# A hybrid decoder trunk on one core: two sets of rotation tables, later reads of table accumulators, and three smaller reorderings

## The chip, the cores and the metric

The kernel runs on one core of a Trainium2 chip. The metric is the device time of one execution in microseconds (us). The median of three runs is 2419.24 us (2417.57 to 2420.35).

## What is computed

Two streams of tokens go through two layers that share one set of weights: a prompt (16 meta tokens and 1024 tokens) and a sample (8 sequences of 8 tokens, which bring caches). Layer 0 mixes with a diagonal complex scan (S5) beside sliding-window attention, layer 1 with a convolution module; each layer ends in a gated feed-forward block.

```python
def s5_mixer(u, h0_re, h0_im, lam_re, lam_im, log_step, b_re, b_im, c_re, c_im, d_skip, w_glu, b_glu):
    ...
    decay = jnp.exp(lr * dt)
    a_re = decay * jnp.cos(li * dt)
    a_im = decay * jnp.sin(li * dt)
    ...
    _, _, hr, hi = lax.associative_scan(_complex_affine_combine, (a_full_re, a_full_im, bu_re, bu_im), axis=1)
    y = (jnp.einsum('ntgp,gcp->ntgc', hr, c_re.astype(f32))
         - jnp.einsum('ntgp,gcp->ntgc', hi, c_im.astype(f32)))
    y = y.reshape(n, t, D_SSM) + d_skip.astype(f32) * uf
    g = jax.nn.gelu(y)
    out = g * jax.nn.sigmoid(g @ w_glu.astype(f32) + b_glu.astype(f32))
    return out.astype(u.dtype), hr[:, -1], hi[:, -1]

def trunk(x, ssm_re, ssm_im, swa_k, swa_v, conv_st, ffn_st, p):
    for layer in range(DEPTH):
        h = rmsnorm(x, p['g_mix'][layer])
        if layer % 2 == 0:
            z = h @ p['w_in_mix'][idx]
            ...  # u, q, k, v = parts of z; ya = s5_mixer(u), yb = sliding-window attention(q, k, v)
            x = x + jnp.concatenate([ya, yb.astype(ya.dtype)], axis=-1) @ p['w_out_mix'][idx]
        else:
            yc, nc = conformer_conv(h, past, ...)
            x = x + yc
        h = rmsnorm(x, p['g_ffn'][layer])
        yf, nf = conv_ffn(h, past, ...)
        x = x + yf
    return rmsnorm(x, p['g_final']), states
```

All matrices are 32-bit. The S5 part has 32 groups of 16 channels with 64 complex states each; D_MODEL is 1024.

## The kernel before

**Tiling.** The tokens stand along the free axis, 512 in stream A and 592 (528 of prompt, 64 of sample) in stream B. A projection is a row of units: one block of weight columns times one stream, summed in the accumulator `pu` (TensorE, L329). To keep 32-bit accuracy each operand is cut into a high and a low half, and each step of a unit takes three products (high by high, low by high, high by low). A weight block is loaded by SyncE into one of four `raw` buffers, its high half `whi` is made by ScalarE (L224) and its low half `wlo` by VectorE (L230), in five slots that come free as TensorE finishes with them. Units of A (inputs `a0h`, `a0l`, ...) and of B (`y0h`, ...) alternate over the same weights.

**What sets the order.** There is no scheduler: each engine does its instructions in the order in which the program was written, and waits at the head of its queue. `run` goes through the units, and after each step of a unit calls `pump`, which advances deferred stages by one tick (`chain`, `tick`) and lets background generators go some steps further, each at a rate of its own. The generators that matter here run beside the first projection (the one that makes u, q, k, v) and behind it:

- `s5_rot` makes four groups (j = 0 to 3) of rotation tables, cosine and sine of an angle. For each: GpSimd adds the angles into `tz` (L755), ScalarE takes their absolute value and two sines (L759 to L761), VectorE multiplies (L763), ScalarE squares and scales (L765, L766), and SyncE stores the two tables `tj` to the memory buffer `tD` (L768). There is one set of `tz` halves and of `tj` tables for all four groups.
- `s5_prep` makes the other tables, again for j = 0 to 3: `ee` (L834 to L839) and `ff` (L854 to L859) on VectorE, a product into the accumulator `psk` (L876) that ScalarE copies to `kz` (L880), with a diagonal that VectorE adds (L882) and a store to `mD`, and two transposes into `psf` (L890) that ScalarE copies to `xf` (L893) and SyncE stores to `xfD`.
- attention, block by block: queries come back through memory (`xB<-qD`), scores `sps` (L1246), scaled by VectorE into `xA` (L1250), maximum `mx` and `nm` (L1190, L1192), exponentials on ScalarE (L1197).
- `s5_main`, behind them: loads of `u`, `xf`, the tables `T`, `m`, `e`; `stage1` (products and a rotation), `stage2` (two scans with the decay rows `dk`, rotation back into `H`, then end states `hf` and initial states copied by ScalarE, L973 and L975), `stage3` (products into `yps`). The output goes to memory and is read back as `yrd` for the gate.

`qst` (L553) and `us` (L1425) are VectorE's reads of finished accumulators `pu`: queries and S5 channels. A third unit can start in an accumulator only when the first has been read, since there are two.

Two more places: the sample's attention multiplies by its values in two groups of four sequences (L1410 with 128 cached rows, L1411 with 8 new rows, alternating), and `start_norm` lets a background generator make the norm of a stream: after `wait` steps it forms the sums of squares (`psum_s`, L381), the reciprocal roots (L366 to L373), and spreads them (`psum_r`, L402).

Of the kernel before, what the change touches and what calls it, by code (L numbers as in the profile page):

```python
# [19 lines left out]
P = 128  # L20
# [107 lines left out]
class Trunk:  # L128
    def __init__(self, ctx, tc, a, o):
# [7 lines left out]
        self.now = self.nt = 0  # L137
# [52 lines left out]
    def bank(self, name="bk"):  # L190
        return self.psb.tile([P, 512], F32, tag="b", name=name)

# [526 lines left out]
    def s5_rot(self):  # L719
# [31 lines left out]
        y = tz[:, 0:576].rearrange("p (g q b) -> p g q b", g=4, q=9)  # L751
        c = tz[:, 576:1152].rearrange("p (g q b) -> p g q b", g=4, q=9)
        for j in range(4):
            g4 = slice(4 * j, 4 * j + 4)
            G.tensor_tensor(y, ta[:, g4, :].unsqueeze(2).to_broadcast([P, 4, 9, 16]),  # L755
                            tb[:, g4, :].unsqueeze(3).to_broadcast([P, 4, 9, 16]), op=OP.add)
            yield
            tcos, tsin = (pp.tile([P, 4, 9, 16], F32, name="tj", tag=f"tj{ri}") for ri in range(2))
            nc.scalar.activation(c, y, AF.Abs)  # L759
            nc.scalar.activation(c, c, AF.Sin, bias=hpi, scale=-1.0)  # L760
            nc.scalar.activation(tcos, y, AF.Sin)  # L761
            yield
            nc.vector.scalar_tensor_tensor(tsin, tcos, 2.0, c, op0=OP.mult, op1=OP.mult)  # L763
# [3 lines left out]
            for ri, tt in ((1, tsin), (0, tcos)):  # L767
                nc.sync.dma_start(self.dq(self.tD, ri, j, 132), tt.rearrange("p g q b -> p g (q b)")[:, :, 0:132])  # L768
# [5 lines left out]
    def s5_prep(self):  # L774
# [86 lines left out]

        nxt = table_e(0)
        yield
        for j in range(4):
# [9 lines left out]
            for gi in range(4):  # L874
                for ri in range(2):
                    nc.tensor.matmul(ps[gi * 32:(gi + 1) * 32, 0:P], bd[:, ri, gi, :],  # L876
                                     ee[:, ri, gi, 0:8, :], start=(ri == 0), stop=(ri == 1))
            z = self.t_tile(240, "kz")
            V.memset(z[:, 0:112], 0.0)
            nc.scalar.copy(z[:, 112:240], ps[:, 0:P])  # L880
            dcol = self.pc["ssm_d"] + j
            V.scalar_tensor_tensor(z[:, 112:128], mask16, self.pt[:, dcol:dcol + 1], z[:, 112:128],  # L882
                                   op0=OP.mult, op1=OP.add)
            nc.sync.dma_start(dap(self.mD, 8 * j * 16 * 8 * P, [[8 * P, P], [P, 8], [1, P]]),
                              dap(z, 0, [z.ap[0], [16, 8], [1, P]]))
            yield
            for ri in range(2):
# [5 lines left out]
                nc.scalar.copy(xf, ps)  # L893
                nc.sync.dma_start(dap(self.xfD, ri * 16 * P + 4 * j * P, [[32 * P, P], [1, 512]]), xf)
                yield


    def s5_main(self, gA):
# [15 lines left out]
        for i in range(2):  # L914
            nc.gpsimd.memset(d_(i)[:, :, 0:1], 0.0)
# [95 lines left out]
        for i in range(10):  # L1011
# [15 lines left out]
            if i >= 2:  # L1027
                load_m(i)
                load(i, e_, self.eD, P)
# [1060 lines left out]
```

## Time and profile before

| | before |
|---|---|
| median of three runs | 2419.24 us |
| profiled execution | 2420.04 us |
| its span | 2418.3 us |
| TensorE (PE) busy | 2319.7 us, 96% |
| VectorE (DVE) busy | 1662.1 us, 69% |
| ScalarE (ACT) busy | 995.0 us, 41% |
| GpSimd (POOL) busy | 136.9 us, 6% |
| the chain that ended last | PE 79%, DVE 10%, ACT 5%, DMA 4% |

A share of busy time is an average over the span: TensorE's is between 0.6 and 0.9 in the first eighth of it, and 0.9 or more behind. What matters is in which stretch an engine stood still, and what ended that. The mean granted TensorE clock of the whole execution is 0.977 of full speed.

### The profile page before, as it was taken

The numbers are of one execution on the slowest core, as the hardware profiler recorded it, in microseconds if no ns is written. First come the engines' busy times: TensorE is split into PE (matmuls) and PEld (weight loads), VectorE is DVE, ScalarE is ACT, GpSimd is POOL, SyncE is SP. The second block draws the span as 40 slices with busy tenths as digits, with TensorE's granted clock in tenths as the row PEclk, the third lists the DMA queues.
The fourth block names the chain that finished last, engine by engine and source line by source line (L and its number), as shares of the span: only waits on it lengthen the run. The fifth ranks groups of instructions, "written<-read, shape, count | busy, mean of one in ns | idle before, by whom it ended". The sixth has DMA issues, their size and how long they took to land.

```text
span 2418.3 us, 37176 instructions
## 1 busy us (share of the span) xinstructions
PE 2319.7 (96%) x13896; PEld 2084.7 (86%) x13896; DVE 1662.1 (69%) x3049; ACT 995.0 (41%) x1903; POOL 136.9 (6%) x380
## 2 busy tenths in 40 slices
PE   7688899999999999999999999999999999999998
PEld 5567778677887878999999999888887989999998
DVE  7768565554678688888887478898988564344443
ACT  6433444654434343423336333443335444233333
POOL 4001300000000001000000000000000000000000
PEclk8899999999999999999999999999999999999999
DMA  7777734224333423222222432333332423222222
GB/s 217 194 138 194 208 121 154 74 75 126 89 97 106 138 83 92 82 81 82 77 79 83 140 106 79 98 95 103 94 99 77 133 86 96 80 79 79 83 80 70
DMA packets 455354, 257.82 MB, mean 107 GB/s; under 512 B 57323, under 2 KB 446599, under 8 KB 453222
## 3 DMA queue, kind: packets, MB, share of 16 engines
q1 hardware_dynamic: 451990, 251.55, 36.1%
q0 software_dynamic: 2496, 2.68, 0.4%
q8 instruction: 110, 1.80, 0.3%
q10 hardware_dynamic: 688, 1.21, 0.1%
q14 instruction: 70, 0.57, 0.1%
HBM read 223.05 MB, written 35.59 MB: 107 GB/s over the span
## 4 chain that ended last, share of the span: by engine, by line
PE 79%; DVE 10%; ACT 5%; DMA 4%; issue 2%; SPq 0%; ACTq 0%; POOL 0%; DVEq 0%
PE pu L329 75%; DVE wlo L230 2%; DMA yrd<-yD 1%; ACT whi L224 1%; PE tps L1233 1%; DVE xB L1686 1%; DMA raw<-in_w_in_mix 1%; ACT P L1197 1%; DVE mx L1190 1%; PE sps L1246 0%; DVE hf L417 0%; DMA xbD<-xB 0%; PE psum_s L381 0%; PE ops L1260 0%; DVE cv L1517 0%
## 5 line engine op out<-in xcount | busy, mean ns | idle before, releaser
L230 DVE TENSOR_TENSOR wlo<-raw,whi 128x512 fp32r<-128x512 f32 x712 | 481.2, 679 | 498.6 <-ACT whi L224 486.1
L224 ACT CAST whi<-raw 128x512 fp32r<-128x512 f32 x712 | 428.4, 607 | 682.9 <-PE pu L329 630.9
L1686 DVE SCALAR_TENSOR_TENSOR xB<-gl,pt,xB 128x528 f32<-128x528 f32 x240 | 183.1, 763 | 4.3 <-ACT xB L1680 2.9
L1686 DVE SCALAR_TENSOR_TENSOR xA<-gl,pt,xA 128x512 f32<-128x512 f32 x240 | 179.0, 747 | 3.7 <-ACT xA L1680 1.5
L1506 ACT ACTIVATE cv<-cv 128x608 f32<-128x608 f32 (+2 forms) x88 | 58.9, 670 | 162.4 <-DVE cv L1505 162.4
L329 PE MATMUL pu<-a0h,whi 128*128 128x296 f32 (+3 forms) x318 | 92.4, 343 | 14.1 <-ACT G L1486 4.9
L1504 DVE SCALAR_TENSOR_TENSOR cv<-G,pt,cv 128x608 f32<-128x608 f32 (+2 forms) x88 | 70.1, 796 | 45.9 <-ACT cv L1503 45.8
L329 PE MATMUL pu<-a4h,whi 128*128 128x296 f32 (+3 forms) x306 | 88.8, 341 | 12.2 <-DVE xA L460 9.6
L329 PE MATMUL pu<-a2h,whi 128*128 128x296 f32 (+3 forms) x318 | 90.9, 339 | 0.0
L329 PE MATMUL pu<-a1h,whi 128*128 128x296 f32 (+3 forms) x318 | 90.5, 338 | 0.0
L329 PE MATMUL pu<-a3h,whi 128*128 128x296 f32 (+3 forms) x318 | 90.1, 337 | 0.0
L329 PE MATMUL pu<-a0l,whi 128*128 128x296 f32 (+3 forms) x318 | 90.1, 337 | 0.0
L329 PE MATMUL pu<-a1l,whi 128*128 128x296 f32 (+3 forms) x318 | 89.9, 336 | 0.0
L329 PE MATMUL pu<-a1h,wlo 128*128 128x296 f32 (+3 forms) x318 | 89.8, 335 | 0.0
L329 PE MATMUL pu<-a0h,wlo 128*128 128x296 f32 (+3 forms) x318 | 89.6, 335 | 0.0
L329 PE MATMUL pu<-a2h,wlo 128*128 128x296 f32 (+3 forms) x318 | 89.6, 334 | 0.0
L329 PE MATMUL pu<-a2l,whi 128*128 128x296 f32 (+3 forms) x318 | 89.5, 335 | 0.0
L329 PE MATMUL pu<-a3l,whi 128*128 128x296 f32 (+3 forms) x318 | 89.0, 333 | 0.0
L329 PE MATMUL pu<-a3h,wlo 128*128 128x296 f32 (+3 forms) x318 | 88.7, 332 | 0.0
L329 PE MATMUL pu<-a6h,whi 128*128 128x296 f32 (+3 forms) x306 | 88.2, 339 | 0.0
L329 PE MATMUL pu<-a6l,whi 128*128 128x296 f32 (+3 forms) x306 | 87.1, 336 | 0.9 <-DVE a6l L230 0.9
L329 PE MATMUL pu<-y0h,whi 128*128 128x296 f32 (+2 forms) x236 | 67.5, 342 | 21.2 <-DVE kz L882 17.2
(650 smaller groups left out, 6238.8 us busy)
## 6 DMA issues: line engine op xcount, KB each, us to landing
raw<-in_ffn_w_up SPq DMA_DIRECT2D x352, 256.0 KB, 2.9
raw<-in_ffn_w_down SPq DMA_DIRECT2D x128, 256.0 KB, 2.8
raw<-in_conv_w_pw SPq DMA_DIRECT2D x96, 256.0 KB, 2.8
raw<-in_ffn_w_down SPq DMA_DIRECT2D x64, 192.0 KB, 2.5
xbD<-xB SPq DMA_DIRECT2D x3, 2368.0 KB, 9.8
xB<-xbD SPq DMA_DIRECT2D x6, 1184.0 KB
raw<-in_w_in_mix SPq DMA_DIRECT2D x16, 256.0 KB, 5.8
raw<-in_w_in_mix SPq DMA_DIRECT2D x32, 128.0 KB, 3.5
```

The costliest lines, as they stand in the source:

```text
L224: nc.scalar.copy(hi, src)
L230: nc.vector.tensor_tensor(lo, src, hi.bitcast(F32), op=OP.subtract)
L329: nc.tensor.matmul(ps[:, ch, :c], wt, xt[:, off + ch * c:off + (ch + 1) * c], start=(k == 0 and pi == 0), stop=(k == nk - 1 and pi == 2))
L1190: V.tensor_reduce(mx, pt, axis=AX.X, op=OP.max)
L1197: nc.scalar.activation(pt[:, h, :], pt[:, h, :], AF.Exp, bias=nm[:, h:h + 1], accum_out=sm[:, h:h + 1])
L1233: nc.tensor.transpose(v[:, h, :], pt[:, 4 * kv + h, ko:ko + m], self.ident[:nq, :nq])
L1504: nc.vector.scalar_tensor_tensor(c, G[:, 1:1 + n], wc(1), c, op0=OP.mult, op1=OP.add)
L1506: self.chain(lambda: None, lambda: None, lambda: nc.scalar.activation(c, c, AF.Gelu_apprx_tanh))
L1686: V.scalar_tensor_tensor(acc, gl[:, i:i + npp], w(i), acc, op0=OP.mult, op1=OP.add)
```

## The change

Five edits.

1. `s5_rot` uses two sets of tables in turn. The sum of the angles goes into one half of `tz`, which is also where the second sine and the product end up; the cosine table is `tj0` or `tj1`, by j. ScalarE takes the first sine ahead of the absolute value. Two more steps of the generator stand in each j, so that every part of a later table comes later in the program.
2. `kz` and `xf` are copied out of their accumulators one tick later (`later_read`), and the diagonal of `kz` with its store three ticks after that. The `kz` buffers are two fixed ones, whose zeros are written once by GpSimd. `bank` lets ticks pass if a deferred read still holds an accumulator that comes round.
3. In `s5_main` the first column of `H` is zeroed once by GpSimd, the decay rows `dk` of an iteration are copied at its end, and the end states of an iteration are copied in the next one, behind `stage1`.
4. The sample's value products take the four of 128 rows first, and then the four of 8 rows.
5. The norm of B ahead of layer 0's feed-forward block waits 16 steps and not 7. It lies beside the first projection of A's convolution.

```diff
@@ bank, later_read
+        while self.held and self.nb - min(self.held) >= 4:
+            self.tick()
+        self.nb += 1
         return self.psb.tile([P, 512], F32, tag="b", name=name)
+
+    def later_read(self, lag, read, *more):
+
+        n = self.nb - 1
+        self.held.append(n)
+
+        def f():
+            read()
+            self.held.remove(n)
+        self.chain(*[lambda: None] * lag, f, *more)
@@ s5_rot
-        y = tz[:, 0:576].rearrange("p (g q b) -> p g q b", g=4, q=9)
-        c = tz[:, 576:1152].rearrange("p (g q b) -> p g q b", g=4, q=9)
         for j in range(4):
             g4 = slice(4 * j, 4 * j + 4)
+            y = tz[:, 576 * (j % 2):576 * (j % 2 + 1)].rearrange("p (g q b) -> p g q b", g=4, q=9)
...
-            tcos, tsin = (pp.tile([P, 4, 9, 16], F32, name="tj", tag=f"tj{ri}") for ri in range(2))
-            nc.scalar.activation(c, y, AF.Abs)
-            nc.scalar.activation(c, c, AF.Sin, bias=hpi, scale=-1.0)
+            tcos = pp.tile([P, 4, 9, 16], F32, name="tj", tag=f"tj{j % 2}")
             nc.scalar.activation(tcos, y, AF.Sin)
-            yield
-            nc.vector.scalar_tensor_tensor(tsin, tcos, 2.0, c, op0=OP.mult, op1=OP.mult)
+            nc.scalar.activation(y, y, AF.Abs)
+            nc.scalar.activation(y, y, AF.Sin, bias=hpi, scale=-1.0)
+            yield
+            yield
+            nc.vector.scalar_tensor_tensor(y, tcos, 2.0, y, op0=OP.mult, op1=OP.mult)
+            yield
             yield
             nc.scalar.activation(tcos, tcos, AF.Square)
             nc.scalar.activation(tcos, tcos, AF.Identity, bias=1.0, scale=-2.0)
-            for ri, tt in ((1, tsin), (0, tcos)):
+            for ri, tt in ((1, y), (0, tcos)):
@@ s5_prep
+        zs = pp.tile([P, 2, 240], F32, name="kz", tag="bt")
+        nc.gpsimd.memset(zs[:, :, 0:112], 0.0)
...
-            V.memset(z[:, 0:112], 0.0)
-            nc.scalar.copy(z[:, 112:240], ps[:, 0:P])
...
+            self.later_read(1, lambda z=z, ps=ps: nc.scalar.copy(z[:, 112:240], ps[:, 0:P]),
+                            lambda: None, lambda: None, diag)
...
-                nc.scalar.copy(xf, ps)
...
+                self.later_read(1, out)
                 yield
+        self.flush()
@@ s5_main
+            nc.gpsimd.memset(h_(i)[:, :, :, 0:1], 0.0)
...
-            nc.scalar.copy(dk[:, :, 1:], self.r8[:, g0:g0 + 2].unsqueeze(2).to_broadcast([P, 2, NKP - 1]))
...
-            V.memset(H[:, :, :, 0:1], 0.0)
...
+            if 1 <= i < 9:
+                ends(i - 1)
             if i >= 2:
                 ys = self.t_tile(4 * NK, "ys").rearrange("p (g k) -> p g k", g=4)
                 stage3(i - 2, ys)
...
+            if i < 8:
+                decay(i)
@@ the sample's attention
-            for b in range(4):
-                bs = slice(32 * b, 32 * b + 32)
-                out = ps[:, b].rearrange("p v j t -> p (v j t)")
-                nc.tensor.matmul(out, vc[:, b, :], t[:, 0:2, bs], start=True, stop=False)
-                nc.tensor.matmul(out, vn[:, b, :], t[:8, 2:4, bs], start=False, stop=True)
+            for m, v, w in ((P, vc, t[:, 0:2]), (8, vn, t[:8, 2:4])):
+                for b in range(4):
+                    nc.tensor.matmul(ps[:, b].rearrange("p v j t -> p (v j t)"), v[:, b, :],
+                                     w[:, :, 32 * b:32 * b + 32], start=(m == P and b == 0), stop=(m == 8),
+                                     skip_group_check=True)
@@ run
-        add(lambda: self.start_norm(B, "g_ffn", 0, "a", pB))
+        add(lambda: self.start_norm(B, "g_ffn", 0, "a", pB, 16))
```

ScalarE's order around the exponentials of attention blocks 0 (`xA`, 128x128) and 1 (128x256), before; the first three `tz`/`tj` rows are the sines of table 3, `whi` a weight's high half:

```order
L224 CAST whi<-raw 128x512
L759 ACTIVATE tz<-tz 128x576
L760 ACTIVATE tz<-tz,hpi 128x576
L761 ACTIVATE tj<-tz 128x576
L1197 ACT_TABLE_LOAD
L1197 ACTIVATE xA,smx<-xA,nm 128x128 x8
L1198 ACTIVATE es<-es 128x8
L844 COPY bd<-bb 64x8x16 x2
L224 CAST whi<-raw 128x512
```

The same place after the change, from block 0's exponential to block 1's:

```order
L1230 ACTIVATE xA,smx<-xA,nm 128x128 x8
...
L914 COPY xf<-psf 128x512
L772 ACT_TABLE_LOAD
L772 ACTIVATE tj<-tz 128x576
L773 ACTIVATE tz<-tz 128x576
L774 ACTIVATE tz<-tz,hpi 128x576
L914 COPY xf<-psf 128x512
L238 CAST whi<-raw 128x512
L1267 COPY xB<-tps 128x512 x2
L1230 ACT_TABLE_LOAD
L1230 ACTIVATE xA,smx<-xA,nm 128x256 x8
```

The sines of table 3 stood in front of block 0's exponentials; they now stand between the two blocks, with one table load ahead of them and one behind.

VectorE's order where the queries of the unit before (`qst`) and the S5 channels (`us`) are read, before; L763 is the product of the rotation tables 1 and 2:

```order
L763 SCALAR_TENSOR_TENSOR tj<-tj,tz 128x576
L230 TENSOR_TENSOR wlo<-raw,whi 128x512
L553 TENSOR_TENSOR qst<-pu,Rk 128x512
L879 MEMSET kz 128x112
L882 SCALAR_TENSOR_TENSOR kz<-mask_115,pt,kz 128x16
L763 SCALAR_TENSOR_TENSOR tj<-tj,tz 128x576
L1425 TENSOR_TENSOR us<-pu,Rk 128x64x8
L230 TENSOR_TENSOR wlo<-raw,whi 128x512
```

And after, where the product is L777:

```order
L244 TENSOR_TENSOR wlo<-raw,whi 128x512
L567 TENSOR_TENSOR qst<-pu,Rk 128x512
L777 SCALAR_TENSOR_TENSOR tz<-tj,tz 128x576
L899 SCALAR_TENSOR_TENSOR kz<-mask_115,pt,kz 128x16
L1458 TENSOR_TENSOR us<-pu,Rk 128x64x8
L244 TENSOR_TENSOR wlo<-raw,whi 128x512
```

The product of table 1 went from in front of the low half and `qst` to behind them, and that of table 2 left this place.

ScalarE's order in an iteration of `s5_main`, from the copies out of stage 1 (`xs`) to the next iteration's, before:

```order
L949 COPY xs<-xr 128x16
L950 COPY xs<-xi 128x16
L958 COPY dk<-r_813 128x2x129
L973 COPY hf<-H 128x2x2
L975 COPY H<-h_866 128x2x8 x2
L224 CAST whi<-raw 128x512
```

And after, in the second iteration:

```order
L973 COPY xs<-xr 128x16
L974 COPY xs<-xi 128x16
L1002 COPY hf<-H 128x2x2
L1004 COPY H<-h_866 128x2x8 x2
L997 COPY dk<-r_813 128x2x129
L238 CAST whi<-raw 128x512
```

The end states `hf` were copied behind this iteration's decay rows; they are now those of the iteration before, ahead of the rows, and the high half does not stand behind a fresh `H`.

## Rows read from the trace of the kernel before

**Rows 1.** One stretch: us, then busy us of each engine (count), granted clock, DMA share, GB/s.

```profile
82.00:149.00 67.00, 41.16 (x238) 33.24 (x237) 43.06 (x74) 26.28 (x70) 3.12 (x4) 0.82 0.70 147
```

**Rows 2.** The list of waits: engine, line, waited for, us in total, times, longest.

```profile
ACT tj L761 <- DMA tD<-tj: 31.2, 3, 15.2
```

**Rows 3.** TensorE's timeline, 90 to 173 us: start, duration, line, work, [idle before <- releaser].

```profile
91.86 0.83 PE L329 MATMUL pu<-y0h,whi 128*128 128x296 f32 x2 [9.27 <-DVE kz L882]
...
99.95 0.72 PE L1246 MATMUL sps<-kT,xB 64*128 64x128 f32 x8 [1.64 <-DMA xB<-qD]
...
104.17 1.71 PE L1246 MATMUL sps<-kT,xB 64*128 64x128 f32 x8 [2.50 <-ACT xf L893]
...
112.75 1.10 PE L876 MATMUL psk<-ee,bd 128*32 128x128 f32 x16 [3.30 <-DVE xA L1250]
...
122.11 0.51 PE L329 MATMUL pu<-y0h,whi 128*128 128x296 f32 x2 [1.23 <-DVE kz L882]
...
148.72 0.83 PE L329 MATMUL pu<-y0h,whi 128*128 128x296 f32 x2 [6.75 <-DVE kz L882]
...
172.18 0.54 PE L329 MATMUL pu<-y0h,whi 128*128 128x296 f32 x2 [1.03 <-DVE us L1425]
```

**Rows 4.** ScalarE's timeline, 113 to 138 us.

```profile
113.59 0.68 ACT L761 ACTIVATE tj<-tz 128x576 f32<-128x576 f32 x1 [5.78 <-DMA tD<-tj]
114.29 1.28 ACT L1197 ACT_TABLE_LOAD   x1
115.58 0.40 ACT L1197 ACTIVATE xA<-xA,nm 128x128 f32<-128x128 f32 x1
...
125.83 0.62 ACT L224 CAST whi<-raw 128x512 fp32r<-128x512 f32 x1 [1.60 <-PE pu L329]
...
137.37 0.51 ACT L1197 ACTIVATE xA<-xA,nm 128x256 f32<-128x256 f32 x1 [9.76 <-DVE nm L1192]
```

**Rows 5.** VectorE's timeline, 84 to 148 us.

```profile
84.35 0.76 DVE L839 SCALAR_TENSOR_TENSOR ee<-ee,x 128x576 f32<-128x576 f32 x1
...
91.04 0.68 DVE L553 TENSOR_TENSOR qst<-pu,Rk 128x512 f32<-128x512 f32 x1
...
120.79 1.17 DVE L1425 TENSOR_TENSOR us<-pu,Rk 128x592 f32<-128x592 f32 x1
...
147.41 1.16 DVE L1425 TENSOR_TENSOR us<-pu,Rk 128x592 f32<-128x592 f32 x1
```

**Rows 6.** TensorE's timeline at the sample's value products, 577 to 587 us.

```profile
577.79 0.33 PE L1410 MATMUL ops<-PT,xB 128*128 128x64 f32 x2
...
580.59 0.50 PE L329 MATMUL pu<-a1h,whi 128*128 128x512 f32 x1
...
586.45 0.63 PE L329 MATMUL pu<-a5h,whi 128*128 128x512 f32 x1
```

**Rows 7.** TensorE around B's norm sums; the last row is from the chain.

```profile
853.21 2.26 PE L381 MATMUL psum_s<-ones,acc 128*128 128x1 f32 x10 [3.15 <-DVE acc L434]
...
855.91 0.63 PE L329 MATMUL pu<-y0l,whi 128*128 128x512 f32 x1
...
859.32 0.40 PE L329 MATMUL pu<-y3h,whi 128*128 128x512 f32 x1
...
860.48 0.40 PE L329 MATMUL pu<-y4h,wlo 128*128 128x512 f32 x1
...
1383.98 1.01 PE psum_s L381 x10
```

**Rows 8.** The scan, 204 to 288 us: TensorE, ScalarE, SyncE, TensorE.

```profile
204.00 1.19 PE L937 MATMUL xr<-u,xf 128*64 128x138 f32 x8 [6.27 <-DMA u<-uD]
...
267.79 0.20 ACT L973 COPY hf<-H 128x4 f32<-128x4 f32 x1 [3.70 <-DVE H L972]
...
269.62 0.58 SPq L241 DMA_DIRECT2D raw<-in_ssm_w_glu  x1
...
287.19 0.77 PE L329 MATMUL pu<-a4h,whi 128*128 128x512 f32 x1 [8.44 <-DVE xA L460]
```

More of the change, by code (lines that the diff above doesn't have):

```diff
@@ L136, in __init__ @@
         self.nbuf = {}
-        self.now = self.nt = 0
+        self.now = self.nt = self.nb = 0
+        self.held = []
     def pools(self):
@@ L877, in s5_prep, with diag @@
                                      ee[:, ri, gi, 0:8, :], start=(ri == 0), stop=(ri == 1))
-            z = self.t_tile(240, "kz")
-            V.memset(z[:, 0:112], 0.0)
-            nc.scalar.copy(z[:, 112:240], ps[:, 0:P])
[L881 to L885, printed above, removed]
+            z = zs[:, j % 2]
+            def diag(z=z, j=j):
+                dcol = self.pc["ssm_d"] + j
+                V.scalar_tensor_tensor(z[:, 112:128], mask16, self.pt[:, dcol:dcol + 1], z[:, 112:128],
+                                       op0=OP.mult, op1=OP.add)
+                nc.sync.dma_start(dap(self.mD, 8 * j * 16 * 8 * P, [[8 * P, P], [P, 8], [1, P]]),
+                                  dap(z, 0, [z.ap[0], [16, 8], [1, P]]))
+            self.later_read(1, lambda z=z, ps=ps: nc.scalar.copy(z[:, 112:240], ps[:, 0:P]),
+                            lambda: None, lambda: None, diag)
             yield
@@ L892, in s5_prep, with out @@
                 xf = self.t_tile(512, "xf")
-                nc.scalar.copy(xf, ps)
-                nc.sync.dma_start(dap(self.xfD, ri * 16 * P + 4 * j * P, [[32 * P, P], [1, 512]]), xf)
+                def out(ri=ri, j=j, ps=ps, xf=xf):
+                    nc.scalar.copy(xf, ps)
+                    nc.sync.dma_start(dap(self.xfD, ri * 16 * P + 4 * j * P, [[32 * P, P], [1, 512]]), xf)
+                self.later_read(1, out)
                 yield
+        self.flush()
     def s5_main(self, gA):
@@ L972, in stage2, with decay, ends @@
             V.tensor_tensor(hr, hr, t1, op=OP.subtract)
+        def decay(i):
+            nc.scalar.copy(d_(i)[:, :, 1:], self.r8[:, 2 * i:2 * i + 2].unsqueeze(2).to_broadcast([P, 2, NKP - 1]))
+        def ends(i):
+            g0, H = 2 * i, h_(i)
             nc.scalar.copy(self.hf[:, :, g0:g0 + 2], H[:, :, :, NKP])
```

## The prediction

> **What bounds the kernel now.** TensorE is busy for 96% of the span, and the chain that ended last is 79% TensorE, so only stretches in which TensorE stands still or runs at its lower clock can give time. I read the busy shares by slice first. They fall early, so next came the windows there: from 82 to 149 us TensorE works 41.16 of 67 us at a mean granted clock of 0.82, with DMA at 0.70 and no other engine full [rows 1]. Something orders this stretch badly. TensorE's own instructions there name the stops: the B halves of three projection units start at 91.86, 122.11 and 148.72 after 9.27, 1.23 and 6.75 us, and between them it waits 1.64 us for a transfer, 2.50 for ScalarE and 3.30 for VectorE [rows 3]. The release put down to VectorE's kz at 91.86 is really the accumulator read qst before it: qst ended at 91.72 [rows 5], and another B half started 0.15 us after the same kind of read. Behind qst stands ScalarE. The list of waits has ScalarE waiting 31.2 us in three pieces for a table's store, because the next sine may not overwrite tj before it has left [rows 2]; the third of them is the 5.78 us at 113.59 [rows 4]. Weight halves queue behind that sine. Two stops lie elsewhere: around 580 us (products with 8 rows between products with 128) and at 853 us (B's norm sums) [rows 6, 7].
>
> **The change, part by part.** *Two sets of tables.* I followed the stretch by hand.
>
> First, the B half of unit 0. The product L763 of j = 0 leaves its place in front of VectorE's first ee group, and goes behind qst; the second ee group therefore ends as before, at 84.35 + 0.76 = 85.11 [rows 5]. The wait of the sine is gone, so a low half (about 0.6) and qst (0.68) follow at once, to 86.4, and the B half starts at 86.5, 5.4 us earlier.
>
> Second, up to the B half of unit 1. The score product at 99.95 waited for xB, which came 8.2 us after qst's end at 91.72 [rows 3, 5]. From 86.4 that is 94.6; SyncE now has the second eD pair and a tD pair ahead of it, so I take 96, a gain of 4.0 and not 5.4. After it, 2.50 (a table copy behind the sine), 3.30 (scores that VectorE scaled behind a table group which now starts some 15 us earlier) and about 1.0 of the 1.23 go. Between 104 and 118 us TensorE ran at its lower level after these waits. Some 16 products there cost 0.195 us each more, 0.427 against 0.232 for a step, both read from [rows 7]: eight steps in 3.41 us, then five in 1.16, which is 3.1. Sum 4.0 + 2.5 + 3.3 + 1.0 + 3.1 = 13.9: that B half starts at 108.2.
>
> Third, to the B half of unit 2 something is given back. Its start was set by VectorE: from us at 120.79 to us at 147.41 [rows 5], and the low half between them waited for a high half at 125.83, itself 1.60 us late for a TensorE slot [rows 4]. The slot now frees at 108.2 + 3.6 = 111.8. But the sine of table 3 now stands between the exponentials of attention blocks 0 and 1, so ScalarE has to do, from 108.1 on: waiting for the product (0.75, as long as a table pass of VectorE at 84.35 [rows 5]), Square and Identity (2 x 0.68, as the sine at 113.59), a copy (0.6, as the high half at 125.83), **a table load** (1.28, at 114.29), sine, absolute value, sine (3 x 0.7), a copy (0.6) [rows 4]. That ends at about 114.8, three us after the slot. The second added load, back to the exponential, falls into ScalarE's idle 9.76 us before 137.37 [rows 4] and costs nothing; without that cover it would be 1.28. So of the 13.9 about 3.1 go back: **10.8**. Bounds: if xB comes no earlier than now, 6.8, and 6 if the second load shows too; if the slot and not the sine releases the high half, 13.9.
>
> The row at 114.29 shows the price of a switch: the sine before it ended at 114.27, the load ran 1.28, the exponential began at 115.58 [rows 4], 1.31 from end to start. The Trainium skill, "ScalarE: Activation LUTs" (section "What ACT_TABLE_LOAD costs"), puts 1.38 us of draining on top of the 1.28. That speaks against this part of the change; by it the give-back would be 4.5 and the time 1.4 longer. This row shows no drain, so the sum takes 1.28.
>
> *Later reads of kz and xf.* ScalarE's copies come one step later and kz's diagonal three more, out of the way of us. That kz is zeroed once on GpSimd saves four small memsets on VectorE, beside other work: nothing. For table 3 it lets us go in front of a kz that waited for ScalarE: the 1.03 at 172.18 [rows 3] goes. **1.0**, from 0 if us waits for its accumulator anyway.
>
> *Decay rows and end states.* ScalarE waited for H in front of the end-state copies eight times (3.70 at 267.79 [rows 8]), with a weight's high half behind them. Moved one iteration on, the copies find H ready. Seven of the eight fall where TensorE stands still for nothing, and give nothing. The eighth counts: high half, low half, then the raw load at 269.62, on whose queue the next read of the scan's output stands; the unit that needs it starts at 287.19, after 8.44 us [rows 8]. Without H that low half ends at about 267.2 and not 268.9: **1.7**. Nearest bounds are 0 (if the read waits for its own data) and the whole 3.7.
>
> *The 8-row products.* Each of two groups takes eight products in 580.59 - 577.79 = 2.80 us, 0.35 each [rows 6]; products of this size in an unbroken run take 0.72 / 8 = 0.09 (the scores at 99.95) [rows 3]. I put the difference on the change of rows. After: two changes at 0.36 and six steps at 0.09, 1.26 a group, 2 x 1.54 = 3.1. From 586.45 on eight steps run at the lower level [rows 6]; with half as long a thin stretch I expect the level to hold, 8 x 0.195 = 1.6, less 0.3 for the group's end. **4.4**. Bounds 1.2 (half of the steps' saving, level still falls) and 4.7.
>
> *B's norm sums.* At 853.21 TensorE waited 3.15 us for the last sum of squares, then took 2.26 us at the lower level, and eight steps from 855.91 to 859.32 took 3.41 us where 8 x 0.232 = 1.86 is full speed; the same ten instructions took 1.01 at 1383.98 [rows 7]. Moved behind a whole projection unit and one step (some 6 us later), the sums find their input ready and the engine at its upper level: 3.15 + 1.25 + 1.55 + 0.25 for the first step = **6.2**. The reciprocal roots then come about 2 us later on VectorE; the normalized B is wanted only after all of this convolution's projections. Bounds 3.15 (the wait alone) and 6.3.
>
> **Rivals.** (a) *The front part is paid back before 204 us.* At 204.00 TensorE waits 6.27 us for u [rows 8], a transfer. If that were due at a fixed time, 10.8 + 1.0 would vanish there, and 4.4 + 6.2 + 1.7 = 12.3 remain: 2407.7 on the profile. Against: u stands in SyncE's queue behind a raw load that waits for a low half, which itself follows the last softmax; all of it moves with TensorE. DMA speaks for it a little: 0.70 x 67 = 47 us of transfers would sit in 56, a share of 0.84.
> (b) *Slower: ScalarE is stopped by the other set.* With two sets the add on GpSimd for table j waits for the store of table j - 2. Should that store be late, the sine stops ScalarE just as now, with the softmax and the weight halves behind it, at j = 2 and at j = 3. Two stops as long as the worst now (15.2 [rows 2]) cost 30.4: 2420.0 - 24.1 + 30.4 = 2426. It decides from 14.5 us of lateness each (29 = 24.1 + 4.9). By my schedule store 0 is issued near 77 and its sine stands at about 92, store 1 near 97 and its sine at 112: margins of 15 us, where the holds of before were 5.8 to 15.2 in all [rows 2, 4].
> (c) *The levels stay low.* If ops and norm save only waits and steps (1.2 + 3.15) and the stretch 6.8, the time is 2420.0 - 6.8 - 1.0 - 1.7 - 4.4 = 2406.
> (d) *The change does not do what it says*: the tables' second set is there, but xB, not the sine, sets units 1 and 2, and the small parts lie beside other waits: within 5 us of before.
>
> **How the numbers follow.** 10.8 + 1.0 + 1.7 + 4.4 + 6.2 = 24.1. The profiled execution took 2420.04 (span 2418.3 and 1.7 around it), 0.8 above the median of the three runs, 2419.24. So 2420.0 - 24.1 = 2395.9 on it, and **2395** on the median's scale. By the page on table loads it would be 2396.5.
> Chances: forecast, 2389 to 2401, 0.62; (c) and mixtures between 2401 and 2406, 0.13; (a), 2406 to 2411, 0.11; more gained (no give-back, bounds at their upper ends: 13.9 + 1.0 + 3.7 + 4.7 + 6.3 = 29.6, or 2390, and more beyond), below 2389, 0.05; (d) 0.05; (b) 0.04. The range 2388 to 2409 holds all of the forecast and (c), most of (a), some 0.82. A measurement of this kernel tells about 0.2% or 4.8 us from no change: faster 0.91, same 0.05, slower 0.04.
>
> **What would show it.** Right: no wait of a sine for tD; the second projection's B halves near 86.5, 108 and 138; two more table loads of 1.28 us; the last TensorE wait before the third B half still long, about 10 us, and put on us or a low half. Groups of 8-row products near 1.3 us with no fall of the granted clock behind them; the norm sums at about 1.0 us without a wait. Wrong: TensorE's wait for u longer than 6.27 by what the front part gained, stores landing after their sine, or the granted clock still 0.66 around the moved sums.

## The result, and the profile after

The changed kernel takes 2394.53 us (median of four runs, 2390.43 to 2397.86) against 2419.8 us of the kernel before in the same comparison: a ratio of 0.9897 with a 95% interval of 0.9884 to 0.9909. The forecast was 2395 with a range of 2388 to 2409. The profiled execution took 2396.57 us with a span of 2394.4 us, and its mean granted clock is 0.984 of full speed where it was 0.977.

How far TensorE is ahead of the kernel before, at the places that the forecast names, is the first thing to read. Both columns are starts of the same instruction in the two profiled executions.

| place | before | after | ahead |
|---|---|---|---|
| B half of unit 0 | 91.86 | 86.86 | 5.0 |
| B half of unit 1 | 122.11 | 108.31 | 13.8 |
| B half of unit 2 | 148.72 | 138.31 | 10.4 |
| end of the wait for u | 204.00 | 191.84 | 12.2 |
| the start behind the read of the scan's output | 287.19 | 275.28 | 11.9 |
| first 8-row group | 577.79 | 562.92 | 14.9 |
| nine projection steps behind the second group | 590.02 | 571.92 | 18.1 |
| first unit of the convolution, its B half's start | 843.14 | 826.27 | 16.9 |
| a later unit, behind B's norm sums | 869.01 | 846.33 | 22.7 |
| end of the span | 2418.3 | 2394.4 | 23.9 |

Each column is one execution, and such starts move from one execution to the next. In the profiles of the products alone, the norm alone and the ends alone (all below), which change nothing in front of it, the B half of unit 2 starts at 145.60, 147.36 and 146.44, where the kernel before has 148.72. In the two later profiles of the changed kernel it starts at 136.58 and 137.09. So the lead there lies somewhere between 7.3 and 12.1 us.

The stretch of [rows 1] has become this, in a window of the same instructions (us, then busy us of TensorE, its weight loads, VectorE, ScalarE, GpSimd; granted clock, DMA share, GB/s):

```profile
82.00:139.00 57.00, 39.27 (x238) 32.44 (x237) 43.97 (x73) 28.05 (x69) 2.56 (x2) 0.87 0.77 164
```

TensorE does its work of that stretch in 57 us and not 67, and DMA goes from 0.70 to 0.77. The stops of [rows 3] and [rows 8], TensorE's timeline (start, duration, work, idle before and what ended it):

```profile
86.86 0.69 PE L343 MATMUL pu<-y0h,whi 128*128 128x296 f32 x2 [4.60 <-DVE qst L567]
...
94.42 0.71 PE L1279 MATMUL sps<-kT,xB 64*128 64x128 f32 x8 [0.87 <-DMA xB<-qD]
...
108.31 0.83 PE L343 MATMUL pu<-y0h,whi 128*128 128x296 f32 x2 [3.69 <-DVE us L1458]
...
114.56 0.43 PE L343 MATMUL pu<-y3h,wlo 128*128 128x296 f32 x2
...
138.31 0.83 PE L343 MATMUL pu<-y0h,whi 128*128 128x296 f32 x2 [7.42 <-DVE smx L1236]
...
191.84 1.19 PE L961 MATMUL xr<-u,xf 128*64 128x138 f32 x8 [6.16 <-DMA u<-uD]
...
275.28 0.76 PE L343 MATMUL pu<-a4h,whi 128*128 128x512 f32 x1 [8.20 <-DVE xA L474]
```

The starts at 86.86, 108.31 and 138.31 were forecast at 86.5, 108.2 and 137.9. The three waits inside the stretch, 1.64, 2.50 and 3.30, have shrunk to 0.87, nothing and nothing. But the wait in front of unit 1's B half, 1.23 before, has grown to 3.69. The stop in front of 172.18 is gone (its start is at 160.24 now). The stop for u is as long as before (6.16, was 6.27), and so is the one in front of 275.28 (8.20, was 8.44).

VectorE in front of the B halves, and under it the low half of the same place in the kernel before:

```profile
92.32 0.69 DVE L244 TENSOR_TENSOR wlo<-raw,whi 128x512 fp32r<-128x512 f32 x1 [3.80 <-ACT whi L238]
...
107.00 1.16 DVE L1458 TENSOR_TENSOR us<-pu,Rk 128x592 f32<-128x592 f32 x1
...
122.46 0.75 DVE L777 SCALAR_TENSOR_TENSOR tz<-tj,tz 128x576 f32<-128x576 f32 x1
```

```profile
106.44 0.69 DVE L230 TENSOR_TENSOR wlo<-raw,whi 128x512 fp32r<-128x512 f32 x1 [1.04 <-ACT whi L224]
```

From the low half at 92.32 to the end of `us` at 108.16 VectorE works without a stop, as it did from 106.44 to 121.96 in the kernel before. ScalarE, with the rows that answer [rows 4]:

```profile
92.19 0.68 ACT L772 ACTIVATE tj<-tz 128x576 f32<-128x576 f32 x1
...
110.09 0.57 ACT L914 COPY xf<-psf 128x512 f32<-128x512 f32 x1
110.67 1.28 ACT L772 ACT_TABLE_LOAD   x1
111.97 0.68 ACT L772 ACTIVATE tj<-tz 128x576 f32<-128x576 f32 x1
...
114.75 0.62 ACT L238 CAST whi<-raw 128x512 fp32r<-128x512 f32 x1
...
116.55 1.28 ACT L1230 ACT_TABLE_LOAD   x1
126.96 0.51 ACT L1230 ACTIVATE xA<-xA,nm 128x256 f32<-128x256 f32 x1 [9.13 <-DVE nm L1225]
```

No sine waits for a store any more. The first of the two added table loads (110.67) stands between a copy that ended at 110.66 and a sine that began at 111.97: 1.31 from end to start, the load and nothing else. That is the second switch of this case where the Trainium skill's 1.38 us of draining ("ScalarE: Activation LUTs", section "What ACT_TABLE_LOAD costs") does not appear. The second added load (116.55) lies in a wait of 9.13 us. Then the value products and B's norm sums, answering [rows 6] and [rows 7]:

```profile
562.92 2.03 PE L1442 MATMUL ops<-PT,xB 128*128 128x64 f32 x16
564.88 0.50 PE L343 MATMUL pu<-a1h,whi 128*128 128x512 f32 x1
...
571.92 0.39 PE L343 MATMUL pu<-a0h,whi 128*128 128x512 f32 x1
```

```profile
774.61 0.49 PE L1575 MATMUL fps<-ident,fstt 128*128 128x128 f32 x2 [1.18 <-DMA fstt<-in_state_ffn]
...
826.27 0.47 PE L343 MATMUL pu<-y0h,whi 128*128 128x512 f32 x1 [2.06 <-DVE xB L474]
...
828.14 0.63 PE L343 MATMUL pu<-y2l,whi 128*128 128x512 f32 x1
...
839.69 1.17 PE L395 MATMUL psum_s<-ones,acc 128*128 128x1 f32 x10
...
846.33 0.39 PE L343 MATMUL pu<-y0h,whi 128*128 128x512 f32 x1
```

A group of products takes 1.96 us, and the steps behind the second run at the upper level. The ten sums take 1.17 us without a wait. The rows at 774.61 and 828.14 show two things that nobody forecast, a new wait of 1.18 us for a transfer, and a lower level of the clock behind 826.27 (0.63 us for a step, where 0.39 is the upper level's; the granted clock of the 5 us from 826.27 on is 0.67). The rows of before against which the last place is taken are these:

```profile
843.14 0.47 PE L329 MATMUL pu<-y0h,whi 128*128 128x512 f32 x1 [2.09 <-DVE xB L460]
...
869.01 0.39 PE L329 MATMUL pu<-y0h,whi 128*128 128x512 f32 x1
```

### The profile page after: what moved, and what is told of

Read it like the earlier page. It is cut to its first block, busy times and chain, and to the rows that moved or that the text cites. A ratio compares the mean times of both kernels' runs of the same rounds, so it can differ in the third digit from the quotient of the medians.

```text
span 2394.4 us, 37182 instructions
## 1 busy us (share of the span) xinstructions
PE 2304.6 (96%) x13896; PEld 2075.3 (87%) x13896; DVE 1661.2 (69%) x3037; ACT 997.8 (42%) x1905; POOL 136.8 (6%) x383
## 4 chain that ended last, share of the span: by engine, by line
PE 80%; DVE 8%; ACT 4%; DMA 2%; issue 2%; SPq 0%; ACTq 0%; DVEq 0%; POOL 0%; POOLq 0%
PE pu L343 76%; DVE wlo L244 2%; ACT whi L238 1%; DMA fstt<-in_state_ffn 1%; PE tps L1266 1%; DVE xB L1719 1%; ACT P L1230 1%; DVE mx L1223 1%; PE sps L1279 0%; PE yps L1009 0%; DMA yrd<-yD 0%; DMA xbD<-xB 0%; DVE hf L431 0%; PE ops L1293 0%; DVE cv L1537 0%
## 5 line engine op out<-in xcount | busy, mean ns | idle before, releaser
L343 PE MATMUL pu<-a7h,whi 128*128 128x296 f32 (+3 forms) x306 | 87.8, 338 | 0.0
```

The lines of the kernel that those rows point to most:

```text
L343: nc.tensor.matmul(ps[:, ch, :c], wt, xt[:, off + ch * c:off + (ch + 1) * c], start=(k == 0 and pi == 0), stop=(k == nk - 1 and pi == 2))
```

## The experiments

Several edits that touch different places make one sum. So each was run on the kernel before by itself, and variants of the changed kernel took the disputed steps apart. They were measured in three further comparisons, and kernels of the same comparison share the runs of the kernel before. Its median was 2415.15 us in the first two of them and 2416.08 in the third, some 4 us under that of the first one; why is not known. A gain in us below is the ratio's, taken of that median; the difference of the medians is up to 1.4 us away from it, and the intervals reach 2 to 4 us to either side.

**The changed kernel again**, as a base:

> The changed kernel once more, as the base for the other runs of this call. Both theories: about 2394 to 2395 us, ratio to the kernel before 0.990; third B half of the first projection at 138.3 us.

2394.78 us, ratio 0.9917 (0.9902 to 0.9931): 20.0 us under before (16.7 to 23.7), where the first comparison had 24.9 (22.0 to 28.1). The changed kernel stands where it stood (2394.53 in the first), and what moved is the kernel before.

**The rotation tables alone** (edit 1 of the change on the kernel before):

> The kernel before with the rotation tables of the change alone (two sets, later steps). Theory (the wait of the sines for the table's store was the cause): the third B half starts near 138.5 us instead of 148.7, TensorE is 10 us ahead from there on, and the time is 10 to 11 us under before, about 2409. Rival (the later copies of kz and xf are needed as well, since ScalarE would now wait for those accumulators): less than half of it, 2415 or more.

2405.87 us, ratio 0.9964 (0.9951 to 0.9976): 8.7 us (5.8 to 11.8). TensorE's second and third B half and the start at which the kernel before had waited 1.03:

```profile
107.53 0.83 PE L329 MATMUL pu<-y0h,whi 128*128 128x296 f32 x2 [4.07 <-DVE us L1426]
...
137.32 0.83 PE L329 MATMUL pu<-y0h,whi 128*128 128x296 f32 x2 [5.99 <-DVE kz L883]
...
160.69 0.54 PE L329 MATMUL pu<-y0h,whi 128*128 128x296 f32 x2 [1.04 <-DVE us L1426]
```

The third B half is 11.4 us earlier than in the profile of the kernel before (8.3 earlier than the earliest of the other three), so the later copies are not needed for this gain: the rival's 2415 falls. The wait in front of the fourth start is still there, 1.04 us. In the changed kernel it is gone, so that one belongs to edit 2.

**Two sets without the later steps:**

> The kernel before with two sets of tables and the sine first, but with the steps of before, so that every instruction keeps its place in the program and no table load is added. Theory (the store's wait was the cause): ScalarE waits for no store, the second B half starts near 87, the second unit's one at 110 to 113 since the high half there stands behind two passes and two copies, nothing is given back to table loads, the third B half near 138 to 140: 9 to 11 us under before. Rival (the later place in the program made the gain): under 4 us.

```diff
+            y = tz[:, 576 * (j % 2):576 * (j % 2 + 1)].rearrange("p (g q b) -> p g q b", g=4, q=9)
...
-            tcos, tsin = (pp.tile([P, 4, 9, 16], F32, name="tj", tag=f"tj{ri}") for ri in range(2))
-            nc.scalar.activation(c, y, AF.Abs)
-            nc.scalar.activation(c, c, AF.Sin, bias=hpi, scale=-1.0)
+            tcos = pp.tile([P, 4, 9, 16], F32, name="tj", tag=f"tj{j % 2}")
             nc.scalar.activation(tcos, y, AF.Sin)
+            nc.scalar.activation(y, y, AF.Abs)
+            nc.scalar.activation(y, y, AF.Sin, bias=hpi, scale=-1.0)
             yield
-            nc.vector.scalar_tensor_tensor(tsin, tcos, 2.0, c, op0=OP.mult, op1=OP.mult)
+            nc.vector.scalar_tensor_tensor(y, tcos, 2.0, y, op0=OP.mult, op1=OP.mult)
```

2409.36 us, ratio 0.9972 (0.9963 to 0.9981): 6.8 us (4.6 to 8.9), less than the 9 to 11 that were expected and more than the rival's 4. TensorE, and ScalarE ahead of the first exponentials:

```profile
110.59 0.83 PE L329 MATMUL pu<-y0h,whi 128*128 128x296 f32 x2 [3.85 <-DVE kz L881]
...
139.65 0.83 PE L329 MATMUL pu<-y0h,whi 128*128 128x296 f32 x2 [6.75 <-DVE kz L881]
```

```profile
99.22 0.69 ACT L758 ACTIVATE tj<-tz 128x576 f32<-128x576 f32 x1 [5.34 <-POOL tz L754]
...
103.66 0.40 ACT L1196 ACTIVATE xA<-xA,nm 128x128 f32<-128x128 f32 x1 [0.91 <-DVE nm L1191]
```

The third B half comes 9.1 us earlier than in the profile of the kernel before (6.0 earlier than the earliest of the other three), with each group of instructions in its old place and no added table load. So the store's wait was the cause of most of the gain. What the later place adds, 2.3 us at that start and 1.9 in the time, is within the spread of single executions and of the intervals. ScalarE's row at 99.22 shows what the changed kernel's rival (b) was about: the sine of table 3 stands 5.34 us for GpSimd's sum, which waits for the store of table 1. Here the stop falls into a wait for the maximum that follows anyway, of which 0.91 us are left at 103.66. It is about a third of the 14.5 us that would have been needed twice to turn the sign.

**Table 3 behind the high half** (the changed kernel with two more steps in front of table 3):

> The changed kernel with table 3 begun two steps later, so that its table load and sines stand behind the weight's high half and the copies of the transposed probabilities, still ahead of block 1's exponentials. Theory (the high half at 114.75 is held up by the load and the sines): high half near 112, third B half near 135.4, 2.9 us faster than the changed kernel in the same call. Rival (VectorE's own chain or the second load sets that B half): no difference, 138.3.

```diff
         for j in range(4):
+            for _ in range(2 if j == 3 else 0):
+                yield
```

2392.53 us, ratio 0.9904 (0.9889 to 0.9920), against 0.9917 of the base. The medians are 2.3 us apart, and the intervals overlap, so the time alone decides nothing. Its trace, and under it that of the base, second and third B half:

```profile
107.71 0.64 PE L343 MATMUL pu<-y0h,whi 128*128 128x296 f32 x2 [4.20 <-DVE us L1460]
...
135.90 0.83 PE L343 MATMUL pu<-y0h,whi 128*128 128x296 f32 x2 [6.76 <-DVE us L1460]
```

```profile
106.75 0.83 PE L343 MATMUL pu<-y0h,whi 128*128 128x296 f32 x2 [3.53 <-DVE us L1458]
...
136.58 0.83 PE L343 MATMUL pu<-y0h,whi 128*128 128x296 f32 x2 [7.43 <-DVE smx L1236]
```

The way from one to the other is 28.19 us and not 29.83: 1.6 shorter, where 2.9 was expected. ScalarE shows why:

```profile
112.99 0.62 ACT L238 CAST whi<-raw 128x512 fp32r<-128x512 f32 x1 [2.17 <-PE pu L343]
```

The high half now waits for TensorE's slot, at 112.99. But these two traces differ in more than the place of the load. First, TensorE's lower level behind the second B half ends sooner in this one: the granted clock of the 6.2 us from there on is 0.72, and 0.55 in the base. The slot comes 0.2 us after the start of the step y3h,wlo, which lies 5.08 us behind the second B half here, and 6.07 in the base. Second, the edit also takes VectorE's product of table 3 (0.66 us, at 122.46 in the first profile of the changed kernel) out of the way between the high half and the reading `us`. Together these are the 1.6.

Two further profiles, of the kernel "both later" below, have table 3 in this place too, and a lower level that lasts as long as the base's. There, as here, the high half waits for nothing but the slot:

```profile
113.06 0.62 ACT L238 CAST whi<-raw 128x512 fp32r<-128x512 f32 x1 [3.13 <-PE pu L343]
```

```profile
113.55 0.62 ACT L238 CAST whi<-raw 128x512 fp32r<-128x512 f32 x1 [2.98 <-PE pu L343]
```

It starts 6.42 and 6.28 us behind the second B half. In the three profiles of the changed kernel it starts 6.44, 6.27 and 6.31 behind it, in each 0.2 us after the start of y3h,wlo (114.56 and 114.75 in the first). So in the changed kernel the slot comes no earlier than the sines and the copy behind them end, and the load and the sines hold back the high half by at most 0.1 us. They did hold it back, by 0.9 us, in the changed kernel without edit 3 (below), whose lower level ended sooner (granted clock 0.72). Behind the high half the way to the third B half is 22.9 us in all kernels with table 3 later, and 23.6 in the changed kernel: the product.

**The 8-row products alone** (edit 4):

> The kernel before with the 128-row products ahead of the 8-row ones alone. Theory (the trace of the changed kernel): each group takes 1.96 us and not 2.80, since only a pass that follows a change of rows costs 0.09 more than 0.112, and the eight steps at the lower level behind them go: 2 x 0.84 + 1.55 = 3.2 us. Forecast's term: 4.4, with groups of 1.26. Rival (the level falls anyway): 1.7.

2412.99 us, ratio 0.9990 (0.9981 to 0.9999), 2.4 us (0.2 to 4.6). The first group, the step behind it and a later step:

```profile
574.59 2.03 PE L1409 MATMUL ops<-PT,xB 128*128 128x64 f32 x16
576.55 0.50 PE L329 MATMUL pu<-a1h,whi 128*128 128x512 f32 x1
...
583.59 0.39 PE L329 MATMUL pu<-a0h,whi 128*128 128x512 f32 x1
```

1.96 us a group, no fall of the level behind them, and 3.2 us more ahead over this stretch (577.79 - 574.59 = 3.20 in front, 590.02 - 583.59 = 6.43 behind), as in the changed kernel. With the old order the level fell behind the groups in four of five profiles; in that of the two sets without later steps it held (granted clock 1.00), and the way from the first group to the last row's step is 10.66 us there and not 12.23. With the new order it fell in none of eight.

**The norm alone** (edit 5):

> The kernel before with the norm of B waiting 16 steps alone. Theory: the stop of 3.15 us goes, the ten instructions take about 1.1 us, and the granted clock does not fall behind them: TensorE is 6.2 to 6.4 us further ahead at the end of that unit than in front of it, and the time is some 6 us under before. Rival (the level falls near there anyway, from the waits in front of it): 4.4 us.

2408.98 us, ratio 0.9969 (0.9959 to 0.9979), 7.5 us (5.1 to 9.9). TensorE in the unit ahead, and the sums; under it the same step of the unit ahead in the changed kernel's third profile:

```profile
839.69 0.47 PE L329 MATMUL pu<-y0h,whi 128*128 128x512 f32 x1 [2.09 <-DVE xB L460]
...
841.39 0.63 PE L329 MATMUL pu<-y2h,whi 128*128 128x512 f32 x1
...
853.12 1.17 PE L381 MATMUL psum_s<-ones,acc 128*128 128x1 f32 x10
```

```profile
825.23 0.40 PE L343 MATMUL pu<-y2h,whi 128*128 128x512 f32 x1
```

The sums cost 1.17 us without a wait. The level falls here in the unit in front of them, behind the wait of 2.09 us at 839.69, as in the first profile of the changed kernel. But it does not always. With the norm moved it fell there in four of eight profiles (granted clock 0.67 over 5.1 us), and in the other four it did not (1.00), behind the same wait. With the norm in its old place it fell behind the sums in all five. Nor does the fall cost what its steps do: eight of them last 1.55 us longer, but two waits later in the same unit, 0.37 and 0.23 us, vanish then, and with the slow starts around them that is 1.1 us. From that unit's start to the later unit of the table the way is 25.87 us in the kernel before, 20.06 in the first profile of the changed kernel, and 19.65 in its third, without the fall. So the edit gives 6.2 us where the level holds and 5.8 where it falls, and the rival, which put the fall at 1.8 us, is right in 0.4 of it.

**Decay rows and end states alone** (edit 3), and **the changed kernel without them**:

> The kernel before with the decay rows and end states moved alone. Forecast: 1.7 us at the start that is at 287.19 in the kernel before. Theory from the two traces: the low half there stands behind H on VectorE, so the read of the scan's output is issued about 1 us earlier and not 1.7, and what counts is when its transfer lands, under a full DMA: between 0 and 1.0 us, TensorE's stop in front of that start stays between 7.4 and 8.5 us.

> The changed kernel without the moved decay rows and end states. Theory (TensorE's stop in front of the start at 275.28 ends when a transfer lands): the read is issued about 1 us later, the stop stays 8 to 9 us, time 0 to 1.5 us above e9_control_again. Forecast's term: 1.7 above. Rival (seven more waits of ScalarE now show, since the front is tighter): 3 us or more above.

Alone: 2414.04 us, ratio 0.9994 (0.9985 to 1.0004). Left out: 2392.66 us, ratio 0.9905 (0.9891 to 0.9919), beside 2396.74 us and 0.9918 (0.9904 to 0.9932) of the changed kernel in the same comparison. Neither shows a gain from this edit; the second points the other way, where 0 to 1.5 us more had been expected, inside the intervals. From the end of the wait for u to the start behind the read, alone and left out:

```profile
202.43 1.19 PE L938 MATMUL xr<-u,xf 128*64 128x138 f32 x8 [6.88 <-DMA u<-uD]
...
286.27 0.77 PE L329 MATMUL pu<-a4h,whi 128*128 128x512 f32 x1 [8.19 <-DVE xA L460]
```

```profile
191.54 1.19 PE L960 MATMUL xr<-u,xf 128*64 128x138 f32 x8 [5.90 <-DMA u<-uD]
...
274.86 0.76 PE L343 MATMUL pu<-a4h,whi 128*128 128x512 f32 x1 [8.29 <-DVE xA L474]
```

The way is 83.8 us with the edit alone and 83.4 in the changed kernel, 83.3 without it in the changed kernel and 83.2 in the kernel before. The read is not issued earlier on that way either: 66.5 us behind the end of the wait for u in the kernel before (270.51 - 204.00), 66.5 in the changed kernel (258.32 - 191.84), 67.4 with the edit alone, 67.3 in the kernel without it. VectorE's rows show where the gain went, first the last of the group that makes H in the kernel before, then the changed kernel:

```profile
267.33 0.42 DVE L972 TENSOR_TENSOR H<-H,d 128x260 f32<-128x260 f32 x1
```

```profile
252.58 0.69 DVE L244 TENSOR_TENSOR a1l<-gt,a1h 128x512 fp32r<-128x512 f32 x1 [1.65 <-ACT a1h L238]
253.19 1.28 DVE L984 TENSOR_TENSOR_SCAN X<-dk,X 128x260 f32<-128x260 f32 x2
...
256.07 0.42 DVE L994 TENSOR_TENSOR H<-H,d 128x260 f32<-128x260 f32 x1
256.41 0.68 DVE L244 TENSOR_TENSOR wlo<-raw,whi 128x512 fp32r<-128x512 f32 x1
```

The low half (256.41) follows H at once, where it stood 1.15 us behind it in the kernel before. But H itself, counted as above, ends 0.9 us later than before (64.7 against 63.8 us; 65.4 with the edit alone, 63.9 without it in the changed kernel): the scan stands behind the low half a1l, which waits for ScalarE, which waits for the read before this one. Of the 1.15 us the low half so keeps 0.3. Then the transfer takes some ten us from issue to use in each (280.54 - 270.51 before, 268.62 - 258.32 after, 9.8 and 9.4 in the other two), whatever the edit.

**Both later** (table 3 as above, and four more steps between the load of the feed-forward state and its transposes), in two comparisons:

> The changed kernel with table 3 begun two steps later (as in e4_sine_later) and the transposes of the feed-forward state four steps later behind their load. Theory: the changed kernel gave back 1.2 us at those transposes because TensorE now reaches them before the load has landed; with the four steps it does not wait, 1.2 to 2.9 us are kept, and with 1.7 from the sine the time is 3 to 4 us under the changed kernel, about 2390 to 2391.5. Rival (the waits only move to the next stop): 2393 or more.

> The changed kernel as the base of this call: 2392 to 2396 us.

> The kernel of e8_both_later beside the changed kernel on the same chip. Theory: no wait at the transposes of the feed-forward state (1.2 to 2.5 us) and a shorter stretch from the second to the third B half (1.7): 3 to 4 us under e9_control_again. Rival (the gains move to the next stop): within 1 us of it.

```diff
-        for _ in range(8):
+        for _ in range(12):
             yield
         ps = self.bank("fps")
```

2391.26 and 2393.26 us, ratios 0.9904 (0.9888 to 0.9919) and 0.9906 (0.9892 to 0.9920). The changed kernel stood at 2394.78 us in the comparison ahead of the first of these and at 2396.74 beside the second, 0.9917 and 0.9918. The transposes have no wait:

```profile
773.01 0.47 PE L1577 MATMUL fps<-ident,fstt 128*128 128x128 f32 x3
```

Both times the medians are 3.5 us apart, as expected, while the intervals of the ratios overlap. The traces do not account for 3.5. The way from the second to the third B half is 29.3 and 29.2 us, 0.5 to 0.8 shorter than the changed kernel's 30.0, 29.8 and 29.9, and not 1.7. And the transposes waited 1.18 and 1.47 us in the first two profiles of the changed kernel, and not in its third. So this version is faster than the kernel before for certain, and perhaps faster than the changed kernel. It does not stand out from the other two variants of it: table 3 later alone has a ratio of 0.9904, and the kernel without edit 3 0.9905.

## Why the prediction was right, and where its steps were not

**The tables: the cause and the size right, the way there not.** The sine's wait for the store was the cause, as the run with two sets alone shows. 10.8 us were forecast and 10.4 measured at the third B half, each of the three starts within 0.4 us, and 8.7 in the time of the tables alone. That the starts agree so closely is luck, for two reasons. Single executions put that lead between 7.3 and 12.1. And two steps failed that the sum hid.

The first is the second B half. The forecast added up TensorE's waits and steps to 13.9 and left 0.2 of the 1.23 us in front of that start. In the trace TensorE is through with the steps before it 16.3 us earlier than before (13.8 + 3.69 - 1.23) and then waits 3.69 us for VectorE's `us`. VectorE sets the start: it works without a stop from the low half at 92.32 on, and that low half came 14.1 us earlier because ScalarE's high half no longer queues behind the sine.

The second is the 3.1 us that go back. ScalarE's chain ended about where it was forecast (high half at 114.75, forecast 114.8), but the slot did not free at 111.8. TensorE ran at its lower level behind the wait of 3.69 us, the stop that the schedule did not have, and the slot came at 114.75 as well. So the loss of 3.4 us from the second to the third B half (30.0 against 26.6) is 2.7 us of a later slot and 0.7 of VectorE's product of table 3. With the table load and the sines out of the way the high half came no earlier, except where the lower level was short. Another sign that the forecast named shows it: TensorE's last wait was to be about 10 us, and is 7.42, because TensorE itself took longer. The sum by the Trainium skill's figure ("ScalarE: Activation LUTs", section "What ACT_TABLE_LOAD costs"), 1.4 us more, is not borne out: this switch too took 1.31 us from end to start.

**Later reads: right.** The 1.03 us in front of 172.18 stands in the runs without edit 2 and is gone with it. Edit 2 was not run alone, so its part of the time is not shown.

**Decay rows and end states: wrong.** The forecast said 1.7 us and the trace says none (12.2 ahead in front, 11.9 behind). The failing step is "Without H that low half ends at about 267.2". On VectorE the low half stands behind the six instructions that make H, which end at 267.75 in the kernel before, so it could come forward only by ScalarE's 1.15 us in between. It did, but H came 0.9 us later, since it hangs on the read before, and the low half kept 0.3. The lower bound of the forecast, 0, is what the runs show. That the full DMA of this stretch sets these reads, and so the stop of eight us, fits the ten us of each transfer, but no run here moved other transfers away from it, so it is argued and not shown.

**The 8-row products: the sign and the place right, the term mis-sized.** 4.4 forecast, 3.2 measured. The group was put at 1.26 us by 0.09 for a product; it takes 1.96, 16 passes of which most stand 0.112 apart. Each product here is two passes where one was counted, and the change of rows costs less than the whole difference. The other part, 1.6 us for a level that holds, came out in full against this profile of the kernel before; in one profile with the old order the level held as well.

**B's norm sums: right.** 6.2 forecast, 5.8 measured in the first profile and 6.2 in the third: the wait, the sums and the eight steps behind them came as forecast. What the forecast did not have is that the level can fall in the unit ahead instead, which costs 0.4.

**What was not forecast.** By the table the parts give 10.4 at the third B half, 1.5 from there to the start at 275.28, 3.2 at the products and 5.8 at the norm, 20.9 us, and the profiled executions are 23.9 apart. The transposes lose 1.2 and the rest of the span behind the norm gains as much. The 3.0 that are left arise between 287 and 577 us, where the change touches nothing. In that stretch the profile of the kernel before took 290.6 us, the longest of all thirteen, which lie between 285.6 and 290.6. The kernel with the moved end states alone is 4.4 us faster there, and that of the norm alone 2.4, which change nothing there either. So most of these 3 us are probably a chance of the single profile of before.

The later comparisons put the change at 20.0 and 19.8 us (16.4 to 23.7 by their intervals). The single edits measured apart, without edit 2, are 8.7 + 2.4 + 7.5 + 1.4 = 20.0, but each of them is known to 2 or 3 us only. So the forecast's 24.1 was probably some 4 us too large: 1.7 for the end states, 1.2 for the products, and the rest not told apart from the noise. It met the first comparison by luck, because the kernel before was measured at 2419.8 there and at 2415 to 2416 later.

Rival (a) fell: the lead at 148.72 was still whole at 204.00, and TensorE's wait for u stayed at 6.16 us. That it did so because the queue in front of the transfer moved with TensorE was the prediction's argument; it fits, and no run tested it apart. Rival (b) fell: the sines of tables 2 and 3 start without a stop in the changed kernel (92.19 and 111.97), and the run with two sets in the old order shows such a stop of 5.34 us that cost the exponentials behind it nothing. Rival (c) fell for the places named; a lower level turned up behind the new wait in front of the second B half, and in half of the profiles in the unit ahead of the norm sums. Rival (d) fell with the time.

## What to carry to other kernels

Where one buffer makes an in-order engine wait for a store, look at everything queued behind that instruction. Here a second set gave 6.8 us (4.6 to 8.9) with nothing else moved. Before costing a wait that is taken away, follow each engine's own order to the step that is late next: a low half that stands behind another group on VectorE gains nothing from a free ScalarE. When an engine's waits go, ask which engine's own work sets the next start: here VectorE's did, and a sum of TensorE's waits met it by chance. And make the sum of a forecast against several runs of the kernel before, for a single profile can carry some microseconds of a lower clock that the change does not touch.

## What the runs showed of the hardware

A switch of tables on ScalarE cost 1.31 us from the end of the instruction before it to the start of the next, in two places. A pass (one of the two instructions that the trace shows for each product of these) of a 64-column product that follows one with another number of rows starts 0.205 us after it, and one that follows its like 0.112 us. TensorE's lower level is not the same from one execution to the next: behind the same wait of 2.1 us ahead of the norm sums the granted clock was 0.67 in four profiles and 1.00 in four, and behind the wait of some 4 us in front of the second B half it was 0.51 to 0.56 over the next 6.2 us in six and 0.72 to 0.77 in three. And eight steps at the lower level, 1.55 us longer, cost 0.4 us where they took the place of waits that followed.
